# One chunk's square blocks over the two halves of the partitions, in place of block-diagonal tiles of two chunks, in a recurrent mixer

## The chip, the cores and the metric

The kernel runs on one core of a Trainium2 chip. A core has a matmul engine (PE, whose weight loads are listed as PEld), three engines for elementwise work (DVE, ACT, POOL), a queue that issues most transfers (SP), 128 partitions of on-chip memory (SBUF) and eight banks per partition for matmul results (PSUM). Each engine runs its own queue in order and waits on semaphores of the others. The metric is device microseconds (us) of one execution, the median of several runs.

## The reference, cut to what matters

A decoder block on 1024 tokens of 1024 columns in fp32: a recurrent mixer (RWKV-7, 8 heads of 64) and a differential attention (4 heads) side by side, merged by gates, then a feed-forward layer that picks 128 of 16384 experts per token. The change touches the recurrence alone:

```python
def step(state, inp):
    r_t, w_t, k_t, v_t, kk_t, a_t = inp
    sa = jnp.einsum('bhvk,bhk->bhv', state, -kk_t)
    state = (state * w_t[:, :, None, :]
             + sa[..., None] * (kk_t * a_t)[:, :, None, :]
             + v_t[..., None] * k_t[:, :, None, :])
    return state, jnp.einsum('bhvk,bhk->bhv', state, r_t)
```

The kernel computes it in chunks of 64 tokens. Within a chunk the recurrence is a unit triangular system with a 64x64 matrix A of decayed products of keys; (1 + A)^-1 turns it into matrix products, and only a 64x64 state passes from chunk to chunk.

## The kernel before, in words

**Stages.** `mix(0)` handles tokens 0 to 511, then `pick(0)` chooses their experts; `mix(1)` and `pick(1)` do the same for tokens 512 to 1023. After that `gates` and `ahead` prepare, and `dense` runs the last 512 tokens through all experts as matrix products. The first 512 tokens go through `peer`: 1024 gathers of 128 expert rows (512 KB each), issued on POOL (L795), each consumed by one DVE instruction (L817 for rows of u, L824 for rows of v). They start during `mix(1)` and go on beside `dense` to the end.

**Inside a mix.** Four calls of `rwkv(h)`, each for two heads: head 0 of the pair has its 64 features on partitions 0 to 63, head 1 on 64 to 127. Beside each call stand the input projections of the next call (matmuls `z`, L162 to L166; their weights are split in two parts by ACT, L147, and DVE, L148), one attention head and four gate columns. The order of each engine's queue is fixed when the program is built: the builder's scheduler lets projections and attention stand between the steps of the recurrence.

**One call of `rwkv`** works on W = 512 tokens: TT = 4 tiles of 128 tokens, NC = 8 chunks of 64. Elementwise products with decays give kt, rr, bT and kT. Then, for each head `hh`:
- `am` (L334, L336): A and its relatives, per 128 tokens a 128x128 product in which only the two diagonal 64x64 blocks are wanted; DVE multiplies with a mask that zeroes the rest (L338), into the tiles mb and mk.
- Diagonal 16x16 blocks of A go out to memory (`m_s`) and back with a block to a partition, DVE inverts them by 30 small steps (L379, L381), the result goes out (`z_s`) and back as the block-diagonal XT (L387). PE transposes it (`xtr`, L390) to X.
- Two doubling levels: DVE masks A (M, L357), PE makes Y (L401), ACT copies it (L403), PE makes Xn and XTn (L409, L414), DVE subtracts them (L410, L415). The two heads alternate, each with a PSUM bank and tiles of its own.
- `akv`, W, U0 (L420, L430), copied by ACT. Then per chunk parity `Pp` and `Qp` (L451 to L457); DVE writes the heads' diagonal blocks (L443) and POOL zeroes the other blocks (L442), so that Pd and Qm are again block diagonal. `rh` and `y` (L462 to L473).
- The state passes through 8 chunks: PE `y` and `sn` (L480, L489), DVE `st` (L490).

Work tiles come from a ring of NR = 22 tiles of 128x512 (`rt`), PSUM results of the mixer from three banks (`rbank`). An instruction that writes a ring tile waits until the last reader of its old contents is done.

In words of size: every fp32 product here appears in the trace as two weight loads and two matmuls; a transpose as one of each.

Of the kernel before, what the change touches and what calls it, by code (L numbers as in the profile page):

```python
# [25 lines left out]
NR = 22  # L26
# [12 lines left out]
PADB = 8 * (16 * P + 16)  # L39
# [6 lines left out]
def body(ctx: ExitStack, tc: tile.TileContext, ins, out, dbg=None):  # L46
# [24 lines left out]

    def at(name, dt=F32):
        return hp.tile([P, 512], dt, name=name, tag="at", bufs=NA)
# [10 lines left out]
    def v4(ap):  # L84
        return ap.rearrange("p (a s) -> p a s", s=P)
# [18 lines left out]
    mask2 = const("mask2", [P, 256])  # L104
    lvl = const("lvl", [P, 2, P])
# [33 lines left out]
    for i in range(4):  # L139
        nc.sync.dma_start(ins["z_s"][i // 2, i % 2].rearrange("(p s) -> p s", p=P), zero[:, 0:4 * PADB // P])  # L140

# [35 lines left out]
    def invroot(ssq, n, scale, eps, op1=OP.add, pool=None):  # L177
        """(ssq * scale + eps) ** -0.5 for [128, n] (op1 max: the larger of the two)."""
# [4 lines left out]
        # a first guess from the exponent, then Newton's steps  # L183
# [16 lines left out]
    def normed(src, w):  # L200
        """RMSNorm of rows of src, w over all partitions (two halves [128, 512] each)."""
# [10 lines left out]
    def to_cols(xn, a, hi, lo):  # L212
        """Rows of 128 tokens (two halves) to the transposed hi, lo [128, column / 128, token]."""
# [9 lines left out]
    def head_stats(sq, W, scale, eps, op1):  # L223
        """Per token and half of the partitions: (sum(sq) * scale, eps) ** -0.5, spread back over them."""
# [13 lines left out]
    def mix(gi, t0, W):  # L238
# [35 lines left out]
        def rwkv(h, kz, rz, vz):  # L274
# [38 lines left out]

            def totok(name, f):
                b = rbank("tt")[:, :W]
                for a in range(TT):
                    nc.tensor.transpose(b[:, a * P:(a + 1) * P], f[:, a * P:(a + 1) * P], ident)
# [4 lines left out]
            # A matrices, all transposed ([s, t]) and block diagonal over the chunks  # L322
            MB = [[None] * TT, [None] * TT]
            MK = [[None] * TT, [None] * TT]
            ATs = [[], []]
            for hh in range(2):
                rs = slice(64 * hh, 64 * hh + 64)
# [703 lines left out]
```

## Time and profile before

| | |
|---|---|
| median of 3 runs | 3668.87 us (3668.75 to 3677.71) |
| profiled execution, first to last instruction | 3659.9 us |
| difference of the fastest run to that span | 8.9 us |
| matmuls on PE, and weight loads | 15166 each |
| busy: PE, DVE, ACT, POOL | 3224.0, 2995.0, 1344.7, 1350.5 us |
| `rwkv` calls of mix(0): decay scan (L290) starts | 89.4, 203.6, 327.2, 452.1 us |
| `rwkv` calls of mix(1) | 835.0, 1010.2, 1188.0, 1362.8 us |
| first gated expert weights of `dense` (L887) | 2175.2 us |

A profile comes from one execution. The page of a profile lists busy time per engine, the span in 40 slices, the chain that ended last and the costliest groups of instructions. Other views list groups by line with the mean time of one, stretches of time with each engine's busy time, or single instructions in order of time. A matmul's listed length includes its way through the array, so neighbours overlap; the distance from start to start is what one costs in a row of many.

### The profile page before, as it was taken

The numbers are of one execution on the slowest core, as the hardware profiler recorded it, in microseconds if no ns is written. First come the engines' busy times: TensorE is split into PE (matmuls) and PEld (weight loads), VectorE is DVE, ScalarE is ACT, GpSimd is POOL, SyncE is SP. The second block draws the span as 40 slices with busy tenths as digits, with TensorE's granted clock in tenths as the row PEclk, the third lists the DMA queues.
The fourth block names the chain that finished last, engine by engine and source line by source line (L and its number), as shares of the span: only waits on it lengthen the run. The fifth ranks groups of instructions, "written<-read, shape, count | busy, mean of one in ns | idle before, by whom it ended". The sixth has DMA issues, their size and how long they took to land. (4 is left out here: it accounts for less than half of the span.)

```text
span 3659.9 us, 46805 instructions
## 1 busy us (share of the span) xinstructions
PE 3224.0 (88%) x15166; PEld 2571.2 (70%) x15166; DVE 2995.0 (82%) x6666; ACT 1344.7 (37%) x2497; POOL 1350.5 (37%) x1100
## 2 busy tenths in 40 slices
PE   6999989998979796678888868999999999999997
PEld 5878867776857675556665656777777777777775
DVE  4655555978889888899988758998999999999997
ACT  3333433343323342122498863322222332222332
POOL 0000000004454445552012223656566665565652
PEclk9988989997979897788989879999999999999998
DMA  4222234426676667886467888999999999999995
GB/s 138 62 72 76 73 109 152 135 79 221 226 239 231 229 235 271 314 319 207 125 207 225 263 282 316 348 340 351 349 356 351 350 351 345 347 340 352 348 351 184
DMA packets 407110, 903.24 MB, mean 247 GB/s; under 512 B 52240, under 2 KB 139088, under 8 KB 402768
## 3 DMA queue, kind: packets, MB, share of 16 engines
q0 software_dynamic: 147456, 536.94, 41.6%
q1 hardware_dynamic: 259408, 363.31, 29.3%
q8 instruction: 119, 1.95, 0.2%
q14 instruction: 127, 1.04, 0.1%
HBM read 831.41 MB, written 68.69 MB: 246 GB/s over the span
## 5 line engine op out<-in xcount | busy, mean ns | idle before, releaser
L795 POOL DMA_INDIRECT uv<-u,ids x512 | 656.7, 1283 | 1140.4 <-DVE uv L817 538.3
L795 POOL DMA_INDIRECT uv<-v,ids x512 | 673.0, 1315 | 582.4 <-DVE acc L824 416.0
L824 DVE SCALAR_TENSOR_TENSOR acc<-uv,act,acc 128x1024 f32<-128x1024 f32 x512 | 655.9, 1281 | 52.4 <-DMA uv<-v,ids 46.0
L817 DVE SCALAR_TENSOR_TENSOR uv<-uv,hb 128x1024 f32<-128x1024 f32 x512 | 617.3, 1219 | 78.2 <-DMA uv<-u,ids 77.2
L147 ACT ACTIVATE whi<-wraw 128x512 fp32r<-128x512 f32 x552 | 344.7, 630 | 741.8 <-PE z L163 252.7
L162 PE MATMUL ua<-fh,whi 128*128 128x512 f32 x1024 | 428.7, 419 | 83.4 <-DVE accd L907 68.2
L148 DVE TENSOR_TENSOR wlo<-wraw,whi 128x512 fp32r<-128x512 f32 x552 | 373.7, 686 | 155.0 <-ACT whi L147 151.3
L163 PE MATMUL ua<-fl,whi 128*128 128x512 f32 x1024 | 422.6, 413 | 0.0
L173 PE MATMUL yk<-vh,ah 128*128 128x512 f32 x768 | 304.3, 396 | 21.7 <-ACT ah L169 20.8
L174 PE MATMUL yk<-vl,ah 128*128 128x512 f32 x768 | 304.3, 396 | 10.8 <-DVE vl L170 10.8
L162 PEld LDWEIGHTS ua<-fh,whi 128*128 128x128 f32 x1024 | 204.5, 200 | 147.5 <-DVE accd L907 85.9
L169 ACT ACTIVATE ah<-gw 128x512 fp32r<-128x512 f32 x128 | 80.8, 631 | 614.0 <-DVE gw L887 614.0
L175 PE MATMUL yk<-vh,al 128*128 128x512 f32 x768 | 304.0, 396 | 0.0
L162 PE MATMUL z<-hh,whi 128*128 128x512 f32 x672 | 273.8, 408 | 1.5 <-ACT whi L147 0.9
L166 PE MATMUL ua<-fh,wlo 128*128 128x512 f32 x1024 | 266.6, 400 | 5.3 <-DVE wlo L148 5.3
L166 PE MATMUL z<-hh,wlo 128*128 128x512 f32 x672 | 270.7, 403 | 0.0
L163 PE MATMUL z<-hl,whi 128*128 128x512 f32 x672 | 270.0, 402 | 0.0
L846 PE MATMUL gb<-oh,ohg 128*128 128x128 f32 x1024 | 226.4, 342 | 40.5 <-ACT ohg L845 39.1
L846 PEld LDWEIGHTS gb<-oh,ohg 128*128 128x128 f32 x1024 | 166.1, 209 | 103.8 <-ACT ohg L845 66.5
L163 PEld LDWEIGHTS ua<-fl,whi 128*128 128x128 f32 x1024 | 204.4, 200 | 44.6
L166 PEld LDWEIGHTS ua<-fh,wlo 128*128 128x128 f32 x1024 | 195.0, 191 | 48.5 <-DVE wlo L148 5.8
L845 ACT ACTIVATE ohg<-ohb,sl 128x128 f32<-128x128 bf16 x512 | 228.1, 537 | 2.5 <-DVE ohb L840 2.4
(325 smaller groups left out, 6199.0 us busy)
## 6 DMA issues: line engine op xcount, KB each, us to landing
wraw<-ut SPq DMA_DIRECT2D x256, 256.0 KB, 6.4
vraw<-v SPq DMA_DIRECT2D x256, 256.0 KB, 6.5
wraw<-w_in SPq DMA_DIRECT2D x168, 256.0 KB, 2.7
gd_s<-st SPq DMA_DIRECT2D x16, 2048.0 KB, 11.2
gt<-gd_s SPq DMA_DIRECT2D x32, 1024.0 KB, 8.9
wraw<-wq SPq DMA_DIRECT2D x64, 256.0 KB, 2.9
g_s<-sgo SPq DMA_DIRECT2D x32, 256.0 KB, 3.1
wraw<-proj SPq DMA_DIRECT2D x32, 256.0 KB, 3.6
```

What stands on the lines that cost most here:

```text
L147: nc.scalar.activation(hi, raw, AF.Copy)
L148: nc.vector.tensor_tensor(lo, raw, hi.bitcast(F32), op=OP.subtract)
L162: nc.tensor.matmul(o, hi, xh(k), start=(k == 0), stop=False)
L163: nc.tensor.matmul(o, hi, xl(k), start=False, stop=False)
L166: nc.tensor.matmul(o, lo, xh(k), start=False, stop=(k == n - 1))
L173: nc.tensor.matmul(o, ah, bh, start=first, stop=False)
L174: nc.tensor.matmul(o, ah, bl, start=False, stop=False)
L175: nc.tensor.matmul(o, al, bh, start=False, stop=last)
L795: nc.gpsimd.indirect_dma_start(out=t, out_offset=None, in_=ins[src], in_offset=bass.IndirectOffsetOnAxis(ap=ids[:, j:j + 1], axis=0))
L817: nc.vector.scalar_tensor_tensor(u, u, 1.0, hb, op0=OP.mult, op1=OP.mult, accum_out=act[:, j:j + 1])
L824: nc.vector.scalar_tensor_tensor(acc, v, act[:, j:j + 1], acc, op0=OP.mult, op1=OP.add)
L846: nc.tensor.matmul(b[:, k * P:(k + 1) * P], o3[:, k], o1[:, k], start=True, stop=True)
```

## The change

The two heads of a call now share every tile. A square block of one chunk and one head takes 64 partitions: chunks of even number on partitions 0 to 63, odd ones on 64 to 127, and the columns hold 64 per pair of chunks and head (q = head x 4 + pair). The zero blocks are no longer stored or multiplied.

- Every 128x128x128 product of the recurrence becomes two products of 64x64x64, one in the upper half of the rows and columns of the array and one in the lower, written in turns (`rs in HC`). `am` has the same number of products, each with 64 weight columns in place of 128. `xtr` is now a product with an identity instead of a transpose.
- In `am` and `byfeat` (Pp, Qp, rh, y) the halves of the rows write to two different PSUM banks; in `each` (xtr, Y, Xn, XTn), `bytok` (akv, W, U0) and the state they write to the two halves of the partitions of one bank.
- Both heads' masks, copies and subtractions are one instruction each. Pd and Qm hold no zero blocks, and POOL's memsets are gone. The chunks' `y` is no longer summed with the state's part in PSUM: it is copied out by ACT and added by DVE.
- The ring has 16 tiles instead of 22, and a second ring `r2` has four tiles of 128x1024 (KR, MB, MK, and the merge's products).
- The scratch `m_s` and `z_s` hold 64x64 blocks; XT comes back in four transfers instead of two.

The matmul, mask and copy shapes shrink as the code below shows; comments taken out elsewhere change nothing.

```diff
-NR = 22
+NR = 16
+NR2 = 4
...
+    def r2(name):
+        return gp.tile([P, D], F32, name=name, tag="r2", bufs=NR2)
...
-            kt, rr = rt_("kt"), rt_("rr")
-            nc.vector.tensor_tensor(c3(kt), c3(kk), Ep[:, :, 0:CH], op=OP.mult)
-            nc.vector.tensor_tensor(c3(rr), c3(rz), Ep[:, :, 1:], op=OP.mult)
+            KR = r2("KR").rearrange("p (k c s) -> p k c s", k=2, s=CH)[:, :, :NC, :]
+            kt, rr = KR[:, 0], KR[:, 1]
+            nc.vector.tensor_tensor(kt, c3(kk), Ep[:, :, 0:CH], op=OP.mult)
+            nc.vector.tensor_tensor(rr, c3(rz), Ep[:, :, 1:], op=OP.mult)
...
+            HC = (slice(0, 64), slice(64, P))
+            QN = 2 * TT
+
+
+            MBK = []
+            for name, src in (("MB", bT), ("MK", kT)):
+                m = r2(name).rearrange("p (q s) -> p q s", s=P)
+                bs = [rbank("am") for _ in HC]
+                for c in range(NC):
+                    for hh, rs in enumerate(HC):
+                        nc.tensor.matmul(bs[hh][HC[c % 2], (c // 2) * P:(c // 2 + 1) * P],
+                                         src[rs, c * CH:(c + 1) * CH], KR[rs, :, c, :], start=True, stop=True)
+                for hh in range(2):
+                    nc.vector.tensor_tensor(m[:, hh * TT:(hh + 1) * TT, :], v4(bs[hh][:, :W]),
+                                            mask2[:, None, :].to_broadcast([P, TT, P]), op=OP.mult)
+                MBK.append(m)
+            MB, MK = MBK
...
-            # A matrices, all transposed ([s, t]) and block diagonal over the chunks
-            MB = [[None] * TT, [None] * TT]
...
+            flat = lambda f: lambda a: f[:, a * P:(a + 1) * P]
+            ctok = totok("ctok", lambda a: kt[:, 2 * a:2 * a + 2, :].rearrange("p c s -> p (c s)"))
...
-            nb = 8 * TT
-            full = lambda t: bass.AP(t.tensor, t.offset, [[P, P], [PADB, TT], [1, P]])
-            diag = lambda t: bass.AP(t.tensor, t.offset, [[16 * P + 16, nb], [P, 16], [1, 16]])
+            nb = 4 * NC
+            full = lambda t, par: bass.AP(t.tensor, t.offset + par * CHB, [[CH, CH], [2 * CHB, TT], [1, CH]])
+            diag = lambda t: bass.AP(t.tensor, t.offset, [[16 * CH + 16, nb], [CH, 16], [1, 16]])
             for hh in range(2):
                 m_s = ins["m_s"][h % 2, hh]
-                for i, mb in enumerate(ATs[hh]):
-                    nc.sync.dma_start(full(m_s)[:, 2 * i:2 * i + 2, :],
-                                      mb.rearrange("p (j k s) -> p j k s", j=2, k=2)[:, :, 0, :])
+                for par, rs in enumerate(HC):
+                    nc.sync.dma_start(full(m_s, par), MB[rs, hh * TT:(hh + 1) * TT, 0:CH])
                 nc.sync.dma_start(ab[hh * nb:(hh + 1) * nb], diag(m_s))
...
-            XT, X = [None, None], [None, None]
+            qv = lambda t: t[:, :QN * CH].rearrange("p (q s) -> p q s", s=CH)
+            XT = qv(rt("XT"))
...
                 nc.sync.dma_start(diag(z_s), z[hh * nb:(hh + 1) * nb])
-                XT[hh] = rt_("XT")
-                nc.sync.dma_start(v4(XT[hh]), full(z_s))
+                for par, rs in enumerate(HC):
+                    nc.sync.dma_start(XT[rs, hh * TT:(hh + 1) * TT, :], full(z_s, par))
+
+            def each(name, l, r):
+
+                b = qv(rbank(name))
+                for q in range(QN):
+                    for rs in HC:
+                        nc.tensor.matmul(b[rs, q, :], l[rs, q, :], r(rs, q), start=True, stop=True)
+                return b
+
+            at_q = lambda t: lambda rs, q: t[rs, q, :]
+            X = qv(rt("X"))
+            nc.scalar.activation(X, each("xtr", XT, lambda rs, q: eyec[rs, :]), AF.Copy)
+            for l in range(2):
+                M = qv(rt("M"))
+                nc.vector.tensor_tensor(M, MB[:, :, 0:CH], lvl[:, l:l + 1, :].to_broadcast([P, QN, CH]), op=OP.mult)
+                Y = qv(rt("Y"))
+                nc.scalar.activation(Y, each("Y", M, at_q(X)), AF.Copy)
+                if l < 1:
+                    nc.vector.tensor_tensor(X, X, each("Xn", XT, at_q(Y)), op=OP.subtract)
+                nc.vector.tensor_tensor(XT, XT, each("XTn", Y, at_q(XT)), op=OP.subtract)
+
+            def bytok(name, l, src, scale):
+                b = rbank(name)[:, :W]
                 for a in range(TT):
+                    for hh in range(2):
+                        for rs in HC:
+                            nc.tensor.matmul(v4(b)[rs, a, HC[hh]], l[rs, hh * TT + a, 0:CH], src[rs, a, HC[hh]],
+                                             start=True, stop=True)
+                t = rt_(name)
+                nc.scalar.activation(t, b, AF.Copy, scale=scale)
+                return v4(t)
+
+            AkV = bytok("akv", MK, vtok, 1.0)
+            Wt = bytok("W", XT, ctok, -1.0)
+            U0 = bytok("U0", XT, AkV, -1.0)
+
+            def byfeat(names, *terms):
+
+                bs = [rbank(names) for _ in HC]
+                o = [b[:, 0:TT * CH].rearrange("p (a s) -> p a s", s=CH) for b in bs]
                 for a in range(TT):
+                    for i, (l, r) in enumerate(terms):
+                        for hh in range(2):
+                            for par, rs in enumerate(HC):
+                                nc.tensor.matmul(o[par][HC[hh], a, :], l[rs, a, HC[hh]], r(rs, a, hh),
+                                                 start=(i == 0), stop=(i == len(terms) - 1))
+                return o
+
...
-                    nc.gpsimd.memset(v4(t)[hc, :, 64 - 64 * hh:128 - 64 * hh], 0.0)
-                    nc.vector.tensor_tensor(v4(t)[hc, :, hc], v4(b)[hc, :, hc], x(hc), op=op)
...
+            halves = lambda t: [t[:, i * TT * CH:(i + 1) * TT * CH].rearrange("p (a s) -> p a s", s=CH)
+                                for i in range(2)]
+            tok = lambda t: lambda rs, a, hh: t[rs, a, HC[hh]]
+            Pd, Qm = halves(rt("Pd")), halves(rt("Qm"))
+            for par, b in enumerate(byfeat("Pp", (Wt, tok(btok)))):
+                nc.vector.tensor_tensor(Pd[par], b, eyec[:, None, :].to_broadcast([P, TT, CH]), op=OP.add)
+            Gp = G.rearrange("p (a c) -> p a c", c=2)
+            for par, b in enumerate(byfeat("Qp", (btok, tok(U0)), (ktok, tok(vtok)))):
+                nc.vector.tensor_tensor(Qm[par], b, Gp[:, :, par:par + 1].to_broadcast([P, TT, CH]), op=OP.mult)
+            by_rr = lambda m: lambda rs, a, hh: m[rs, hh * TT + a, CH:P]
+            for par, b in enumerate(byfeat("rh", (Wt, by_rr(MB)))):
+                nc.vector.tensor_tensor(c4(rh)[:, :, par, :], rr.rearrange("p (a c) s -> p a c s", c=2)[:, :, par, :],
+                                        b, op=OP.add)
...
+            y = rt_("ysb")
+            for par, b in enumerate(byfeat("y", (U0, by_rr(MB)), (vtok, by_rr(MK)))):
+                nc.scalar.activation(c4(y)[:, :, par, :], b, AF.Copy)
+            by = rbank("ys")
...
+                    for rs in HC:
+                        nc.tensor.matmul(by[rs, c * CH:(c + 1) * CH], S[rs, :], rh[rs, c * CH:(c + 1) * CH],
+                                         start=True, stop=True)
...
+                    for rs in HC:
+                        nc.tensor.matmul(b[rs, 0:CH], Pd[c % 2][rs, c // 2, :], S[rs, :], start=True, stop=True)
+                    nc.vector.scalar_tensor_tensor(Sn, b[:, 0:CH], G[:, c:c + 1], Qm[c % 2][:, c // 2, :],
                                                    op0=OP.mult, op1=OP.add)
...
+            o = CH if gi == 0 else 0
+            nc.vector.tensor_tensor(y[:, o:], y[:, o:], by[:, o:W], op=OP.add)
...
+        mg = [r2("mg") for _ in range(4)]
...
-                t = rt_("mg") if i == 0 else sgm
+                t = mg[d // 2][:, d % 2 * 512:d % 2 * 512 + W] if i == 0 else sgm
```

How this moves the queues is seen at two places. The first is PE's queue in the second call of mix(0), from the first doubling level to U0. Rows read: line, operation, result <- operands, shape of the result, and how many in a row; `z` rows are input projections, `pT` attention. Before:

```order
L401 MATMUL Y<-X,M 128x128 x4
L409 MATMUL Xn<-Y,XT 128x128 x4
L414 MATMUL XTn<-XT,Y 128x128 x4
L409 MATMUL Xn<-Y,XT 128x128 x4
L414 MATMUL XTn<-XT,Y 128x128 x4
L401 MATMUL Y<-X,M 128x128 x4
L583 MATMUL pT<-ident,sc 128x128 x4
L401 MATMUL Y<-X,M 128x128 x4
L414 MATMUL XTn<-XT,Y 128x128 x8
L420 MATMUL akv<-vtok,mk 128x64 x8
L430 MATMUL W<-ctok,XT 128x64 x8
L430 MATMUL U_1948<-AkV,XT 128x64 x8
```

The same place of the change, from Y of the first level to U0:

```order
L390 MATMUL Y<-X,M 64x64 x16
L168 MATMUL z<-hl,whi 128x512
L171 MATMUL z<-hh,wlo 128x512
L390 MATMUL Xn<-Y,XT 64x64 x16
L390 MATMUL XTn<-XT,Y 64x64 x16
L390 MATMUL Y<-X,M 64x64 x16
L560 MATMUL pT<-ident,sc 128x128 x4
L390 MATMUL XTn<-XT,Y 64x64 x16
L410 MATMUL akv<-vtok,MK 64x64 x16
L410 MATMUL W<-ctok,XT 64x64 x16
L410 MATMUL U_2066<-akv,XT 64x64 x16
```

Each step has 16 small products for both heads where 4 larger ones for one head stood; the turns between heads (XTn of one beside Xn of the other) are gone, so that each step now stands directly behind the one whose result it needs, with two `z` matmuls or four transposes of the attention between.

The second place is POOL's queue during mix(1), where its gathers (`uv`) stand among its memsets. Before:

```order
L795 DMA uv<-u,ids 128x1024 x2
L292 MEMSET Ep 128x8
L795 DMA uv<-u,ids 128x1024 x33
L442 MEMSET Pd 64x4x64 x2
L442 MEMSET Qm 64x4x64 x2
L442 MEMSET Pd 64x4x64 x2
L442 MEMSET Qm 64x4x64 x2
L795 DMA uv<-u,ids 128x1024 x29
```

The same stretch of the change:

```order
L297 MEMSET Ep 128x8 x5
L773 DMA uv<-u,ids 128x1024 x2
L297 MEMSET Ep 128x8
L773 DMA uv<-u,ids 128x1024 x63
L297 MEMSET Ep 128x8
L773 DMA uv<-u,ids 128x1024 x62
L297 MEMSET Ep 128x8
L773 DMA uv<-u,ids 128x1024
```

The memsets of Pd and Qm, which stood between the gathers, are gone; those of Ep stay. In both orders DVE has consumed 395 of the 1024 gathers when the first gated weights of `dense` stand in its queue.

More of the change, by code (lines that the diff above doesn't have):

```diff
@@ L103, in body @@
     lora = const("lora", [P, 2, 512])
-    mask2 = const("mask2", [P, 256])
-    lvl = const("lvl", [P, 2, P])
+    mask2 = const("mask2", [P, P])
+    lvl = const("lvl", [P, 2, CH])
+    eyec = const("eyec", [P, CH])
     eye16 = const("eye16", [64, 16, 16])
@@ L139, in body @@
     for i in range(4):
-        nc.sync.dma_start(ins["z_s"][i // 2, i % 2].rearrange("(p s) -> p s", p=P), zero[:, 0:4 * PADB // P])
+        nc.sync.dma_start(ins["z_s"][i // 2, i % 2].rearrange("(p s) -> p s", p=P), zero[:, 0:8 * CHB // P])
     def wsplit(src):
@@ L316, in totok @@
                 for a in range(TT):
-                    nc.tensor.transpose(b[:, a * P:(a + 1) * P], f[:, a * P:(a + 1) * P], ident)
+                    nc.tensor.transpose(b[:, a * P:(a + 1) * P], f(a), ident)
                 t = rt_(name)
@@ L416, in rwkv @@
-            b = rbank("akv")[:, :W]
-            for hh in range(2):
-                for a in range(TT):
-                    o = slice(a * P + hh * 64, a * P + hh * 64 + 64)
-                    nc.tensor.matmul(b[:, o], MK[hh][a][:, 0:P], vtok[:, a, hh * 64:hh * 64 + 64],
-                                     start=True, stop=True)
-            AkV = rt_("AkV")
-            nc.scalar.activation(AkV, b, AF.Copy)
-            WU = []
-            for name, src in (("W", ctok), ("U0", v4(AkV))):
-                b = rbank(name)[:, :W]
-                for hh in range(2):
-                    for a in range(TT):
-                        o = slice(a * P + hh * 64, a * P + hh * 64 + 64)
-                        nc.tensor.matmul(b[:, o], XT[hh][:, a * P:(a + 1) * P], src[:, a, hh * 64:hh * 64 + 64],
-                                         start=True, stop=True)
-                t = rt_(name)
-                nc.scalar.activation(t, b, AF.Copy, scale=-1.0)
-                WU.append(v4(t))
@@ L985, in prepare @@
     a["ident"] = np.eye(P, dtype=f)
-    s = np.arange(P)[:, None]
-    t = np.arange(P)[None, :]
-    same = (s // CH) == (t // CH)
-    strict = (same & (t > s)).astype(f)
-    incl = (same & (t >= s)).astype(f)
-    a["mask2"] = c(np.concatenate([strict, incl], axis=1))
+    s = np.arange(P)[:, None] % CH
+    t = np.arange(CH)[None, :]
+    a["mask2"] = c(np.concatenate([t > s, t >= s], axis=1).astype(f))
     lv = []
@@ L995, in prepare @@
     a["lvl"] = c(np.stack(lv, axis=1).astype(f))
+    a["eyec"] = (s == t).astype(f)
+    p = np.arange(P)
+    same = (p[:, None] // CH) == (p[None, :] // CH)
     a["eye16"] = c(np.tile(np.eye(16, dtype=f)[None], (64, 1, 1)))
@@ L1011 @@
            "gd_s": (P // CE, P, 512, CE), "a_s": (NE, P, 512),
-           "m_s": (2, 2, 4 * PADB), "z_s": (2, 2, 4 * PADB)}
+           "m_s": (2, 2, 8 * CHB), "z_s": (2, 2, 8 * CHB)}
 def kernel(**inputs):
```

110 lines of the change are left out of this document (7 added, 103 removed).

## Prediction

> **What bounds the kernel now.** The page first, since it shows the stages: its head and, of its 40 slices of 91.5 us, the busy tenths and the granted clock.
>
> ```profile
> span 3659.9 us, 46805 instructions
> PE 3224.0 (88%) x15166; PEld 2571.2 (70%) x15166; DVE 2995.0 (82%) x6666; ACT 1344.7 (37%) x2497; POOL 1350.5 (37%) x1100
> PE   6999989998979796678888868999999999999997
> DVE  4655555978889888899988758998999999999997
> POOL 0000000004454445552012223656566665565652
> PEclk9988989997979897788989879999999999999998
> ```
>
> PE alone is full in the first six slices (the first mix); from the tenth on DVE is as full, because POOL's gathers need it. The mean over the span hides this, so I cut the span at the starts of the `rwkv` calls (the view of stretches: PE, PEld, DVE, ACT, POOL busy, clock, DMA share, GB/s): four calls of mix(0), two of mix(1), and the dense stage.
>
> ```profile
> 89.00:204.00 115.00, 113.11 (x683) 93.58 (x682) 64.36 (x193) 41.53 (x79) 2.56 (x9) 0.99 0.25 77
> 204.00:327.00 123.00, 118.90 (x673) 98.85 (x673) 63.94 (x192) 40.38 (x77) 2.57 (x9) 0.92 0.24 70
> 327.00:452.00 125.00, 121.45 (x684) 100.45 (x683) 65.60 (x202) 45.92 (x87) 2.57 (x9) 0.92 0.22 68
> 452.00:551.00 99.00, 84.18 (x513) 69.00 (x512) 55.82 (x159) 35.88 (x62) 2.57 (x9) 0.88 0.35 110
> 1010.00:1188.00 178.00, 148.43 (x818) 120.99 (x818) 155.47 (x428) 54.97 (x94) 87.39 (x72) 0.86 0.71 234
> 1363.00:1543.00 180.00, 122.46 (x664) 96.00 (x664) 150.48 (x247) 43.48 (x75) 95.86 (x84) 0.77 0.83 288
> 2200.00:3600.00 1400.00, 1318.70 (x5526) 1052.13 (x5525) 1300.94 (x1729) 410.36 (x709) 820.17 (x619) 0.98 0.95 345
> ```
>
> The first three calls of mix(0) are bound by PE (97 to 98% busy, DVE half idle): what PE sheds there is time won. The fourth has no projections left to fill gaps, 15 of its 99 us are idle on PE. In mix(1) DVE leads (155 of 178 us) and PE follows (148), so DVE's saving counts, at most in full. The dense stage has PE, DVE and the transfers at 93 to 95%; the change does not touch it, and since 395 gathers are consumed ahead of it in both orders, it is not handed more work: what the mixes win arrives at the end.
>
> **The change on PE.** How long a product takes in a row of many is the distance of starts in the view of single instructions:
>
> ```profile
> 136.69 1.06 PE L414 MATMUL XTn<-XT,Y 128*128 128x128 f32 x8
> 137.58 1.06 PE L409 MATMUL Xn<-Y,XT 128*128 128x128 f32 x8
> ...
> 155.71 0.44 PE L471 MATMUL y<-mb,U 128*64 128x128 f32 x4
> 155.93 0.44 PE L473 MATMUL y<-mk,vtok 128*64 128x128 f32 x4
> ...
> L414 PE MATMUL XTn<-XT,Y 128*128 128x128 f32 x256 | 33.4, 278 | 0.0
> ```
>
> Eight instructions with 128 weight columns take 0.89 us, 0.112 each; four with 64 columns 0.22, 0.055 each. The group row is L414 over all calls: 256 = 8 calls x 16 products x 2, so each fp32 product counts twice. Per call, before: am 64, xtr 8, inversion 80, akv/W/U0 48, Pp/Qp 48, together 248 x 0.112 = 27.8 us; rh and y 48 x 0.055 = 2.6; sum 30.4. After: am 64, xtr 32, inversion 160, and three times 96: 544 of 64 columns each. One behind another at 0.055 that is 29.9, no gain. But neighbours now use opposite halves of the rows, and two such streams meet once in the trace, at the end of `am`:
>
> ```profile
> 102.72 0.27 PE L334 MATMUL am<-kt,kT 64*128 64x128 f32 x1
> 102.73 0.37 PE L334 MATMUL am<-kt,bT 64*128 64x128 f32 x1
> ...
> 103.06 0.27 PE L336 MATMUL am<-rr,bT 64*128 64x128 f32 x1
> 103.06 0.27 PE L336 MATMUL am<-rr,kT 64*128 64x128 f32 x1
> 103.17 0.27 PE L336 MATMUL am<-rr,bT 64*128 64x128 f32 x1
> 103.28 0.38 PE L334 MATMUL am<-kt,bT 64*128 64x128 f32 x2
> ```
>
> Products of the two heads start within 0.01 us of each other, and eight matmuls take 0.56 us where a single stream needs 0.90: a factor of 0.62. A 64x64x64 product is not in the trace; its bounds are 0.055 (no overlap) and 0.028 (two full streams). I take 0.055 x 0.62 = 0.034, nearest to that row: 544 x 0.034 = 18.5 us, **11.9 less** per call (0.5 to 15.2). Here the trace shows overlap with two PSUM banks only.
>
> The Trainium skill speaks against part of it: TensorEngine Tiling (Array Packing), Restrictions and Gotchas, says that different row tiles cannot access one PSUM bank at the same time; `each` and `bytok` write both halves to one bank, and no run here shows that. By this rule the sum is that of the first rival below.
>
> The second and third call lose more today:
>
> ```profile
> 98.00:104.00 6.00, 5.53 (x45) 4.80 (x46) 5.54 (x15) 0.69 (x1) 0.00 (x0) 1.00 0.12 34
> 145.00:158.00 13.00, 13.00 (x138) 12.64 (x137) 4.29 (x10) 1.79 (x3) 0.61 (x2) 1.00 0.01 1
> 216.00:222.00 6.00, 6.00 (x29) 6.00 (x29) 2.67 (x5) 0.00 (x0) 0.00 (x0) 0.50 0.20 63
> 222.00:231.00 9.00, 9.00 (x46) 8.78 (x46) 4.50 (x12) 1.47 (x5) 0.00 (x0) 0.50 0.20 47
> ```
>
> There `am` runs at half the granted clock, 75 matmuls in 15 us, 0.2 each: 64 cost 12.8 instead of 7.2. After, at twice 0.034, they cost 4.4 instead of 2.2. So these calls gain 3.4 us more, 15.3.
>
> **What is late next.** Both heads now share each step, so the copy behind a step is no longer covered by the other head's products. Xn stands two projections (about 0.5 us) behind Y, XTn four transposes (0.45) behind the next Y, and the copy takes 0.6 (row of L403 below) plus the way; the second half of `am` waits for a mask (0.69), and Qp, rh and y each for the evacuation of a bank (0.42), as three banks serve products that take two. Six waits of about 0.5: 3 us per call, between 1 and 5. Behind each, PE's whole queue stands, projections too. The transfers around the 16x16 inversion are not in the sum: XT's takes 4.8 us to land, now in four smaller pieces, and projections stand in PE's queue ahead of it as before.
>
> mix(0): 11.9 - 3 = 8.9 for the first call, 12.3 for each of the next two, and for the fourth, where latency rules, half of 11.9: 6. Sum 39 us.
>
> **The change on DVE**, by the groups over all calls:
>
> ```profile
> L357 DVE TENSOR_TENSOR M<-mb,lvl 128x256 f32<-128x256 f32 x64 | 24.2, 421 | 9.3 <-PE Y L401 9.3
> L338 DVE TENSOR_TENSOR mk<-am,mask 128x512 f32<-128x512 f32 x32 | 22.1, 690 | 14.4 <-PE am L336 14.1
> L338 DVE TENSOR_TENSOR mb<-am,mask 128x512 f32<-128x512 f32 x32 | 22.0, 688 | 13.9 <-PE am L336 13.8
> L415 DVE TENSOR_TENSOR XT<-XT,XTn 128x512 f32<-128x512 f32 x32 | 21.8, 684 | 9.9 <-PE XTn L414 9.3
> L490 DVE SCALAR_TENSOR_TENSOR st<-sn,G,Qm 128x128 f32<-128x128 f32 x56 | 19.5, 348 | 33.5 <-PE sn L489 33.1
> L403 ACT ACTIVATE Y<-Y 128x512 f32<-128x512 f32 x32 | 19.0, 595 | 49.0 <-PE Y L401 45.1 <-DVE cand L718 3.9
> L443 DVE TENSOR_TENSOR Pd<-Pp,ident 64x256 f32<-64x256 f32 x32 | 13.5, 422 | 31.2 <-PE Pp L451 30.8
> L443 DVE TENSOR_TENSOR Qm<-Qp,G 64x256 f32<-64x256 f32 x32 | 13.5, 422 | 5.3 <-PE Qp L457 4.8
> L410 DVE TENSOR_TENSOR X<-X,Xn 128x512 f32<-128x512 f32 x16 | 11.0, 684 | 3.2 <-PE Xn L409 3.1
> L442 POOL MEMSET Pd<- 64x256 f32 x32 | 9.8, 306 | 237.1 <-PE Y L401 233.8 <-issue 1.0 <-PE XTn L414 0.7
> XT<-z_s SPq DMA_DIRECT2D x16, 256.0 KB, 4.8
> ```
>
> Per call (an eighth of each count): masks of `am` 8 to 4, 2.8 us saved; M 8 x 0.42 to 2 x 0.69, 2.0; X one and XT two fewer, 2.0; blocks 8 to 4 of 0.42, 1.7; seven `st` of half the width, by the slope between the 256 and 512 columns above 0.07 less each, 0.5. Added: y plus state 0.69, and rh in two pieces of 0.42 for one of 0.69, 0.15. Sum **8.1 us less**. In mix(1) DVE is busy 0.87 of the time, so I count 0.87 x 8.1 = 7 per call, 28 in all (bounds 0, if gathers set the pace, and 12 per call, if PE's saving comes on top). POOL loses its memsets, which held gathers up while they waited; counted in the code, the ring tiles that a call holds at once fall from about 21 to 9, so 16 suffice. Both count as nothing.
>
> **Sum:** 39 + 28 = 67 us. The profiled execution's own time is its span and about 9 us around it, which is the fastest run and, within 0.1 us, the median. 3668.9 - 67 = **3602**; by the bounds of its terms 3570 to 3635.
>
> **Rivals.**
> 1. Halves that share a bank take turns. Then only am and the 192 of Pp, Qp, rh, y overlap: 256 x 0.034 + 288 x 0.055 = 24.5, 5.9 less per call, with 2.5 us of waits: 3.4, 6.8, 6.8 and 3 in mix(0), 20; with 28 in mix(1) 3621. For it: the trace's overlap has two banks. Against it: the halves' results are on different partitions.
> 2. No overlap at all, or PE cannot take instructions faster than one pair in 0.055 us (no stretch of the trace is denser). 29.9 and 2 us of waits against 30.4: mix(0) plus or minus nothing, mix(1) 5 per call from DVE: 3649.
> 3. **Slower: the clock falls.** In rows 216 to 231 PE is listed as fully busy and still has 0.50 for 15 us, with 64-row products and transposes; with 128 rows (145 to 158) it keeps 1.00. If small products hold too little of the array at work, the 480 from xtr to y run at half clock: 480 x 0.068 = 32.6 instead of 23.2, and 3 of waits, less 5 to 8 won in `am`: 4 to 7 lost per call of mix(0), 20 in all; mix(1), with slack, even: 3689. Without overlap too, 480 x 0.11 = 53, 27 lost per call of mix(0) and 15 of mix(1): up to 3840. It decides from a little over half of that stretch at half clock (8.9 won against 16.3 for the whole of it). Against it: 64-row `am` keeps 1.00 in 98 to 104. The Trainium skill, TensorE: Matmul & The Clock Gate, Part 1, has the clock rise after about 3.4 us of sustained work; by that this rival has no room, but the rows of 216 to 231 differ.
> 4. More: full overlap, and mix(1) gains 12 per call: 39 + 13 + 48, 3569 or less.
>
> **Chances.** Forecast 0.49, rivals in order 0.17, 0.15, 0.13, 0.06. A range of 3565 to 3662 holds the first three and most of the fourth case, and leaves out the clock. This kernel's measurement tells about 0.3%, 11 us: faster 0.49 + 0.17 + 0.06 + 0.06 of rival 2 = 0.78, same 0.09, slower 0.13.
>
> **What would show it.** Right: starts of `each` products at about 0.034 us, calls of mix(0) at 105 to 113 us instead of 115 to 125, mix(1) calls at about 170, dense stage as long as before. Rival 1: `byfeat` near 0.034 but `each` at 0.055. Rival 2: all at 0.055. Rival 3: 0.50 in the clock between xtr and y. Wrong altogether: PE idle where XT or the merge's tiles are awaited.

## The result, and the profile after

The changed kernel takes **3570.09 us** (median of 4 runs, 3565.23 to 3577.26) against 3668.81 beside it (4 runs): ratio 0.9736, 95% interval 0.9716 to 0.9757, some 97 us less. Forecast were 3602 us and a range of 3565 to 3662: faster, as forecast, by half as much again as the 67 us of the sum. Two slow executions in the experiments below, 9840 us of `before_turns` and 7760 us of the kernel before, are left out of the ratios.

The head of the page after, with the rows of the 40 slices shown of before:

```profile
span 3564.5 us, 50945 instructions
PE 3102.8 (87%) x17382; PEld 2427.3 (68%) x17382; DVE 2929.3 (82%) x6546; ACT 1335.0 (37%) x2483; POOL 1318.3 (37%) x1036
PE   6999988998888874969888879999989999999997
DVE  4555556977989897899888678999989998999997
PEclk9999988998989886979889989999999999999999
```

PE has 2216 matmuls more and is busy 121 us less; DVE is busy 66 us less, 8.2 per call (forecast 8.1). Cut at the starts of the calls, as before (four calls of mix(0), four of mix(1), `dense`):

```profile
91.30:193.10 101.80, 99.07 (x956) 75.04 (x955) 56.16 (x178) 39.66 (x77) 0.11 (x1) 1.00 0.28 82
193.10:297.70 104.60, 100.26 (x951) 76.90 (x950) 56.51 (x177) 39.52 (x76) 0.11 (x1) 0.95 0.27 78
297.70:402.20 104.50, 99.98 (x959) 76.20 (x958) 57.92 (x187) 43.77 (x84) 0.11 (x1) 0.98 0.26 76
402.20:492.20 90.00, 71.36 (x791) 55.34 (x790) 47.84 (x145) 34.93 (x60) 0.11 (x1) 0.83 0.37 118
774.30:945.90 171.60, 141.67 (x1106) 106.51 (x1105) 143.97 (x416) 54.63 (x94) 78.50 (x62) 0.86 0.71 236
945.90:1110.20 164.30, 134.36 (x1096) 104.06 (x1096) 143.97 (x408) 54.08 (x91) 85.27 (x63) 0.85 0.75 248
1110.20:1269.90 159.70, 133.61 (x1108) 104.20 (x1109) 141.40 (x352) 60.42 (x102) 78.79 (x60) 0.88 0.75 246
1269.90:1440.90 171.00, 100.51 (x904) 75.23 (x903) 134.66 (x221) 40.15 (x71) 92.74 (x75) 0.70 0.84 288
2079.80:3530.30 1450.50, 1363.16 (x5704) 1084.80 (x5705) 1339.32 (x1785) 426.80 (x739) 818.99 (x625) 0.98 0.94 342
```

PE still fills the first three calls, and the second and third now keep 0.95 and 0.98 of the clock instead of 0.92. `dense` is as long as before: 1450.5 us in the last row, against 1449.7 between the same two instructions of the kernel before. Between the profiled executions the spans differ by 95.4 us: mix(0)'s calls give 61.0, mix(1)'s 30.5, all the rest 3.9. A call is counted up to the next call's scan, the fourth up to the merge's first sum.

| call | length before, after | changed products on PE before, after |
|---|---|---|
| mix(0), 1st | 114.2, 101.8 (-12.4) | 30.8, 18.1 (-12.7) |
| 2nd | 123.6, 104.6 (-19.0) | 37.0, 17.7 (-19.3) |
| 3rd | 124.9, 104.5 (-20.4) | 37.0, 17.1 (-19.9) |
| 4th | 99.2, 90.0 (-9.2) | 33.3, 22.4 (-10.9) |
| mix(1), four | 697.1, 666.6 (-30.5) | 144.0, 91.3 (-52.7) |

The last column sums, over am, xtr to U0, Pp, Qp, rh and y, the distances from one matmul's start to the next. In mix(0) each call is shorter by what its products lost on PE, within 1.7 us; in mix(1) little more than half of it arrives. The pace, from the view of single instructions of the first call (start, length, instruction; `each` and `bytok`, whose halves share a bank):

```profile
138.65 1.10 PE L390 MATMUL XTn<-XT,Y 64*64 64x64 f32 x32
139.67 1.15 PE L390 MATMUL Y<-X,M 64*64 64x64 f32 x32
140.75 1.05 PE L573 MATMUL hs<-ones,sq 128*128 128x2 f32 x8
...
144.47 1.15 PE L410 MATMUL W<-ctok,XT 64*64 64x64 f32 x32
145.46 1.04 PE L410 MATMUL U<-akv,XT 64*64 64x64 f32 x30
```

W's 32 instructions take 0.99 us from start to start, **0.031 each**, XTn's 1.02: the overlap that the forecast put at 0.034, and in one bank.

The forecast's bound of 0.028 does not hold where all four quarters of the array take turns, as in `byfeat`. Half of y's instructions in the second call (the other half stand among them), from the views by tile of the changed kernel, of `noturns` (for y: columns in turn, same rows) and of `notile` (one quarter); both are described below:

```profile
L428 PE MATMUL y<-MK,vtok x32: 218/218/265, 250.7 to 251.7; 64*64 64x64 f32 x32
```

```profile
L428 PE MATMUL y<-MK,vtok x32: 218/218/218, 260.3 to 261.8; 64*64 64x64 f32 x32
```

```profile
L428 PE MATMUL y<-MK,vtok x32: 218/218/218, 265.3 to 268.3; 64*64 64x64 f32 x32
```

The 64 instructions of y take 0.99, 1.64 and 3.02 us from start to start: 0.016, 0.026 and 0.047 each. Am, whose products are 128 wide, takes 0.048 each in the first call. On DVE, the groups that answer to those of before:

```profile
L403 DVE TENSOR_TENSOR XT<-XT,XTn 128x512 f32<-128x512 f32 x16 | 11.0, 686 | 13.3 <-PE XTn L390 13.3
L398 DVE TENSOR_TENSOR M<-MB,lvl 128x512 f32<-128x512 f32 x16 | 10.7, 681 | 0.0
L333 DVE TENSOR_TENSOR MB<-am,mask 128x512 f32<-128x512 f32 x16 | 10.2, 681 | 1.5 <-PE am L330 1.5
L438 DVE TENSOR_TENSOR Pd<-Pp,eyec 128x256 f32<-128x256 f32 x16 | 6.0, 418 | 10.7 <-PE Pp L428 10.7
L467 DVE SCALAR_TENSOR_TENSOR st<-sn,G,Qm 128x64 f32<-128x64 f32 x56 | 15.8, 281 | 34.9 <-PE sn L466 34.8
```

XT, MB and Pd have half the instructions at the same length each: one mask takes 0.68 for both heads. M has a quarter, each of twice the width, and st as many, each shorter.

### The profile page after: what moved, and what is told of

Its sections match the earlier page's. It is cut to its first block, busy times and chain, and to the rows that moved or that the text cites. A ratio compares the mean times of both kernels' runs of the same rounds, so it can differ in the third digit from the quotient of the medians.

```text
span 3564.5 us, 50945 instructions
## 1 busy us (share of the span) xinstructions
PE 3102.8 (87%) x17382; PEld 2427.3 (68%) x17382; DVE 2929.3 (82%) x6546; ACT 1335.0 (37%) x2483; POOL 1318.3 (37%) x1036
## 3 DMA queue, kind: packets, MB, share of 16 engines
q14 instruction: 125, 1.02, 0.1%
## 5 line engine op out<-in xcount | busy, mean ns | idle before, releaser
L773 POOL DMA_INDIRECT uv<-u,ids x512 | 644.7, 1259 | 1210.1 <-DVE uv L795 535.9
## 6 DMA issues: line engine op xcount, KB each, us to landing
gd_s<-st SPq DMA_DIRECT2D x16, 2048.0 KB, 11.9
```

The lines of the kernel that those rows point to most:

```text
L773: nc.gpsimd.indirect_dma_start(out=t, out_offset=None, in_=ins[src], in_offset=bass.IndirectOffsetOnAxis(ap=ids[:, j:j + 1], axis=0))
```

## The experiments

Below, "+x us" is the difference of two ratios to the kernel before, times 3669; intervals are 95%, and the changed kernel's own reaches 8 us to each side. Since the builder's scheduler orders the queues anew for each kernel, an edit also moves rows elsewhere: of some 10000 rows of PE in the trace (runs of equal instructions), about 90 differ from the changed kernel's in `memsets`, 600 in `noturns_bank`, 700 to 2500 in the others made from it. Differences of a few us outside the edited place prove nothing.

**Turns of the halves: all, am alone, one bank alone.** Each loop first runs over one half of the rows, then over the other, as in `each`; `noturns` has it everywhere, `noturns_am` in am alone, `noturns_bank` in each and bytok.

```diff
-                for q in range(QN):
-                    for rs in HC:
+                for rs in HC:
+                    for q in range(QN):
```

> The changed kernel with every product loop (am, each, bytok, byfeat) first over all of one half of the rows, then over all of the other; same instructions, same tiles, same work on the other engines. My theory (overlap of the two halves is what PE gains, in mix(0) above all): products go at 0.055 us each instead of 0.03, some 11 to 14 us more of PE per call, the second and third call get their half-clock stretch of about 20 us back; the four calls of mix(0) grow by 10 to 18 us each, mix(1) by 0 to 10 each: 3615 to 3650 us, 45 to 80 over the changed kernel, with PE of a call back near 30 us. Rival A (the gain comes from less work on DVE and POOL): within 10 us of the changed kernel, 3560 to 3580. Rival B (fewer waits, by fewer and larger copies): the same, 3560 to 3585.

> The changed kernel with only am's loop without turns. My theory of the clock (two halves of 64 rows at once are enough for the full clock, one is not): am goes at 0.055 us at full clock in the first call and at about 0.11 us in the second and third, where the half-clock stretch is again near 20 us long instead of 7 or less; these two calls grow by 6 to 12 us each, the first and fourth by 2 to 4: 3585 to 3600 us. Rival (the half-clock stretch went because the work ahead of am moved, not because of am's turns): the half clock stays at 7 us or less, every call of mix(0) grows by 2 to 4 us: 3578 to 3586.

> The changed kernel with only each and bytok (the products whose halves share one bank: xtr, Y, Xn, XTn, akv, W, U0, 288 of 544 instructions per call) without turns; am and byfeat keep theirs. My theory (halves overlap in one bank as they do in two): 288 x (0.055 - 0.03) = 7 us more of PE per call, 15 to 28 us in mix(0), 0 to 15 in mix(1): 3590 to 3610. Rival (in one bank the halves take turns, and the turns win nothing there): no difference, 3563 to 3578.

Measured: `noturns` 3653.62 us, ratio 0.997 (0.9948 to 0.9992), **+86**, a little over the 45 to 80 expected; `noturns_am` 3575.72, 0.9768 (0.9751 to 0.9786), +12, intervals that touch; `noturns_bank` 3655.81, 0.9993 (0.9974 to 1.0013), **+94**, more than twice what was expected. Without the turns of the 288 instructions that share a bank nearly the whole gain is gone, so the rival in which they win nothing is false. So are the rivals of `noturns`, which have the gain from DVE, POOL or fewer waits. Why so much more than pace? Here are `noturns_bank`'s single instructions where W and then U begin, in the second call and in the first:

```profile
269.80 0.27 PE L410 MATMUL W<-ctok,XT 64*64 64x64 f32 x1
271.30 0.27 PE L410 MATMUL U<-akv,XT 64*64 64x64 f32 x1
...
152.67 0.36 PE L410 MATMUL W<-ctok,XT 64*64 64x64 f32 x1
155.35 0.36 PE L410 MATMUL U<-akv,XT 64*64 64x64 f32 x1
```

Without turns W takes 1.50 us, 0.047 each, in the second call, and 2.68 in the first. The stretches of the same run with their clock (third number from the right); its profiled execution is one of its slower ones, 19 us over its median:

```profile
136.00:164.00 28.00, 28.00 (x360) 27.17 (x361) 3.92 (x8) 5.74 (x10) 0.00 (x0) 0.50 0.03 11
252.00:276.00 24.00, 23.35 (x423) 20.28 (x421) 7.92 (x19) 6.11 (x12) 0.00 (x0) 1.00 0.10 27
```

Pace alone lengthens the second and third call by 6.8 and 8.4 us; where the clock falls in the inversion it stays at 0.50 through the chain with PE full, and the first and fourth call lose 21.3 and 15.0. From Y's first start to Qp's last, this run needs 17.8 to 18.4 us in the three calls that keep the clock and 27.7 to 31.8 in the other five, there all but 2 us of it at half clock; the changed kernel needs 11.7 to 17.2, of which at most 8.5 are at half clock, and the kernel before 20.1 to 23.6, all but 2 us of it in one call at full. Three calls of mix(1) are so longer by 17 to 24 us. That is rival 3 of the prediction, which the turns keep away.

`noturns_am` missed from the other side: am lost nothing (2.9 us for 64 in the first call, 3.1 in the changed kernel). The chunks in turn still alternate the halves of the *columns*. That gave the next cut.

**One quarter of the array.** am and byfeat ordered so that neighbours share rows and columns (byfeat likewise by par, then hh):

```diff
-                for c in range(NC):
-                    for hh, rs in enumerate(HC):
+                for hh, rs in enumerate(HC):
+                    for c in [*range(0, NC, 2), *range(1, NC, 2)]:
```

> The changed kernel with am and byfeat (256 of 544 instructions per call) ordered so that neighbours use one quarter of the array, the same rows and the same columns, as each and bytok did in noturns_bank; in noturns, am and byfeat still had neighbours on the other half of the columns and kept their pace. Theory (it is the change of the array's quarter that lets neighbours overlap, by rows or by columns alike): am 64 x (0.10 - 0.045) = 3.5 us more per call, byfeat 192 x (0.048 - 0.026) = 4 us, and the clock falls in some calls: 3600 to 3645. Rival (am and byfeat are not bound by the pace of their products but by banks and copies): 3565 to 3585.

Measured 3608.94 us, 0.9855 (0.9819 to 0.989), **+44**: the theory. Am of the first call, in `noturns_am` (columns in turn) and in `notile`:

```profile
101.20 1.26 PE L330 MATMUL am<-KR,bT 64*64 64x128 f32 x26
...
104.11 0.44 PE L341 MATMUL tt<-ident,KR 128*128 128x128 f32 x2
```

```profile
102.56 2.24 PE L330 MATMUL am<-KR,bT 64*64 64x128 f32 x29
...
107.03 0.44 PE L341 MATMUL tt<-ident,KR 128*128 128x128 f32 x2
```

64 instructions take 2.91 us with columns in turn and 4.47 in one quarter; y takes 3.0 instead of 1.0 to 1.4. In the second call am, and the transposes behind it, stay at half clock for the whole of a stretch of `notile`, 8.3 us for am alone:

```profile
210.30:224.00 13.70, 13.70 (x85) 12.21 (x84) 5.66 (x15) 3.39 (x9) 0.00 (x0) 0.50 0.18 43
```

**The kernel before, with turns.** Am, Pp and Qp write in turns over the row halves, into two banks; 128 weight columns as before. Am's core:

```diff
-                        b = rbank("am")
+                    bs = [rbank("am") for _ in range(2)]
...
+                        for i, x in enumerate((kt, rr)):
+                            for hh in range(2):
+                                rs = slice(64 * hh, 64 * hh + 64)
+                                nc.tensor.matmul(bs[hh][:, 256 * j + 128 * i:256 * j + 128 * i + 128], src[rs, cs],
+                                                 x[rs, cs], start=True, stop=True)
```

> The kernel before, with only am, Pp and Qp in turns over the two halves of the rows (both halves' banks open at once); tiles, masks, inversion and everything else as before. Theory (a turn over tiles of the array that share neither rows nor bank wins the same with 128 columns): am 64 x (0.112 - 0.06) = 3.3 us per call, Pp and Qp 48 x 0.05 = 2.4 us, and the second and third call of mix(0) lose most of the 20.5 us at half clock, 7 us each: mix(0) 35 us shorter, mix(1) 0 to 15: 3610 to 3640. Rival (the overlap needs both halves of the columns as well, products of 128 columns fill them and win nothing): within 8 us of the kernel before, half clock in calls 2 and 3 as before.

Measured 3640.66 us, 0.9903 (0.9866 to 0.994): by the ratio 36 us less than before (22 to 49), at the edge of what was expected. The medians differ by 24 and the profiled spans by 21, so it is a quarter to a third of the change's gain, with none of its tiles. The pace is not where it comes from: only Pp reaches the 0.06 us that was expected (0.062 each), while Qp stays at 0.098, and am hardly shrinks in the first call (6.3 instead of 7.0 us). That call is 3.2 us shorter, the second and third 8.3 and 9.9. In the second the clock is back 4.4 us after am's start at 213.4:

```profile
211.00:217.80 6.80, 6.38 (x35) 4.91 (x36) 4.82 (x14) 1.57 (x5) 0.00 (x0) 0.50 0.23 62
217.80:224.00 6.20, 5.54 (x53) 4.91 (x51) 4.16 (x10) 1.56 (x3) 0.00 (x0) 1.00 0.28 68
```

The stretches at half clock around am of the second and third call, with am's own time:

| kernel | neighbours in am | half clock, us | am, us |
|---|---|---|---|
| before | same rows, all columns | 20.5, 20.5 | 13.3, 13.3 |
| notile | same quarter | 13.7, 13.7 | 8.3, 8.3 |
| before_turns | rows in turn, all columns | 6.8, 3.4 | 8.2, 7.7 |
| noturns_am | columns in turn | 6.8, 6.8 | 4.4, 4.3 |
| changed | rows and columns in turn | 6.8, 3.4 | 4.1, 3.5 |
| memsets (below; PE's loops as changed) | rows and columns in turn | 0, 3.4 | 3.1, 3.6 |

With turns the clock returns while am runs; without, only behind am and tt, though PE is listed as full (the rows above, and 216 to 231 in the prediction).

**What the clock follows.** All lengths in the third column are whole multiples of 3.41 us, and so is each of the 1676 stretches at one clock inside the 14 profiles: the clock changes only on a grid of 3.41 us, which lies differently in each run. What the clock of a window goes with can be read from the window ahead of it. Count each matmul there at 0.112 us per 128 columns of width (0.23 for a projection), times the share of the array's rows and columns that it uses; call the sum array time. Take all windows at half clock in which PE is listed as over 99% busy. With less than 1.0 us of array time, 139 of 161 were followed by half clock again; with 1.4 us or more, 515 of 517 by full clock; between these, 72 of 141. By the same count (an estimate from the rows above) am of the kernel before does 1.7 us in a window at full clock and 0.9 at half, so that once slow it stays slow; `notile`'s does 0.7 at half, `noturns_am`'s 1.4. W does 1.5 us at full clock with turns, 1.0 without, and 0.6 without turns at half clock. So turns win twice, by pace and by the clock that the pace keeps. The counts are an agreement over windows; no run sets where the work lies on the grid.

**Work that holds the clock.** `noturns_bank`, in mix(1) alone with products of 128x128x512 ahead of the steps of the inversion (five before xtr, one before each other), into the bank that the step then overwrites; their results are not used.

```diff
+                for _ in range(0 if gi == 0 else 5 if name == "xtr" else 1):
+                    nc.tensor.matmul(b, blk, lora[:, 0, :], start=True, stop=True)
```

> The kernel of noturns_bank, with additional products of 128 rows, 128 columns and 512 wide, into the bank that the step overwrites after, in mix(1) alone: five ahead of xtr, while XT's transfer is awaited, and one ahead of each later step of the inversion. mix(0) is left as in noturns_bank. Theory (noturns_bank lost half by pace and half by the clock, which single small products do not bring back): the stretches of 40 us and more at half clock go from mix(1)'s inversions, xtr to rh takes 25 us instead of 38 in PE time, and mix(1) is shorter by 15 to 40 us in spite of some 9 us of additional products per call: 3615 to 3640. Rival (the clock only shows the waiting, and the pace is all): the half clock stays or mix(1) is longer by the additional products, 3655 to 3690.

Measured 3657.99 us, 0.9987 (0.9957 to 1.0017; 10 runs from 3631.73 to 3683.05): no difference that can be told. In the profiled execution one of mix(1)'s chains instead of three ran at half clock, which fits the theory; but that execution is the fastest of the ten, 26 us under their median, so whether the extra work costs what the clock wins stays open. This run shows something else, though: PE and DVE run the same instructions in the same order as in `noturns_bank` until mix(1), and yet the first call took 106.0 us against 123.1. The stretch of `noturns_warm`:

```profile
136.00:159.00 23.00, 22.52 (x490) 20.45 (x487) 5.66 (x14) 6.43 (x12) 0.00 (x0) 1.00 0.07 25
```

In `noturns_bank` a window of the grid ends at 136.1, where the half clock begins: it holds xtr's last products, a wait of 0.7 us, Y and the first of pT, 0.8 us of array time. In `noturns_warm` the grid cuts the same instructions elsewhere, and the two windows over them hold 1.4 (projections still among it) and 0.9. That may be the whole difference; it is not shown.

**DVE's saving undone.** Operations that write the same result again, some 8.5 us per call: in `dve_double` where the kernel before had its additional ones (Pd and Qm twice too), in `dve_one` all at the first M (13 times).

```diff
-                for hh in range(2):
+                for hh in (0, 0, 1, 1):
...
-                nc.vector.tensor_tensor(M, MB[:, :, 0:CH], lvl[:, l:l + 1, :].to_broadcast([P, QN, CH]), op=OP.mult)
+                for _ in range(4):
+                    nc.vector.tensor_tensor(M, MB[:, :, 0:CH], lvl[:, l:l + 1, :].to_broadcast([P, QN, CH]), op=OP.mult)
```

> The changed kernel with DVE's saving undone by repeats of operations that write the same result again: per call 4 masks of am (128x512), 6 M (128x512) and 4 blocks of Pd and Qm (128x256), some 8.6 us of DVE, in the places where the kernel before had its additional ones; PE's products unchanged. My theory (mix(1) gains by DVE, mix(0) by PE): mix(1) grows by about 0.87 x 8.6 = 7.5 us per call, 30 in all; in mix(0), where DVE is half idle, the repeats only lengthen the chain behind each step, 0 to 5 us per call: 3595 to 3625, most of it in mix(1). Rival A (DVE is not what bounds mix(1); PE's saving won there): mix(1) grows by less than 8 us in all. Rival B (DVE's saving won in mix(0) too): mix(0) grows by 25 us or more.

> The changed kernel with the same additional work for DVE as in dve_double (12 operations of 128x512, some 8.3 us per call), all in one place: the first level's mask M, written 13 times while XT's transfer is awaited, instead of behind each step of the chain. Theory (DVE's saving counted in mix(0) because it shortens the chain of steps on which PE waits, and in mix(1) because DVE is busy there): mix(0) grows by 0 to 2 us per call instead of the 5.4 of dve_double, mix(1) by 4 to 7 per call: 3585 to 3605. Rival (busy time of DVE is what counts everywhere): as dve_double, 3595 to 3610, of which 20 us in mix(0). Rival (latency alone counts): 3568 to 3580.

Measured: `dve_double` 3601.63 us, 0.9824 (0.9797 to 0.9851), **+32**, within the range, but in the wrong place: by the profile mix(0)'s calls grow by 21.7 us and mix(1)'s by 20.0. Its first calls of mix(0) and of mix(1):

```profile
90.50:198.20 107.70, 104.39 (x956) 78.97 (x955) 63.47 (x191) 39.23 (x76) 0.11 (x1) 0.95 0.26 78
793.90:969.20 175.30, 143.58 (x1107) 108.11 (x1105) 149.67 (x426) 55.05 (x94) 78.15 (x61) 0.83 0.69 228
```

In the first call PE has the same 956 products, is busy 5.3 us longer, and the clock has gone from 1.00 to 0.95: it falls behind a window in which PE waits 1.7 of 3.41 us, against 0.9 us in the changed kernel. `dve_one` missed: 3628.71 us, 0.9886 (0.9866 to 0.9906), +55, with 24 us in mix(0). There Y of the first call starts at 147.5 us instead of 135.5, since M is ready so late, and the order built for it puts projections ahead of Y (DVE's rows, then PE's):

```profile
134.20 7.95 DVE L399 TENSOR_TENSOR M<-MB,lvl 128x512 f32<-128x512 f32 x11
...
145.71 1.41 DVE L399 TENSOR_TENSOR M<-MB,lvl 128x512 f32<-128x512 f32 x2
...
147.21 0.40 PE L167 MATMUL z<-hh,whi 128*128 128x512 f32 x1
147.54 1.15 PE L390 MATMUL Y<-X,M 64*64 64x64 f32 x32
```

So DVE being half idle in mix(0) did not make its work there free: a step that PE's chain waits for counts, wherever it stands. How much of the 55 is the new order and how much the wait stays open.

**POOL's memsets put back**, on ring tiles that nothing reads:

```diff
+            for name in ("Pd", "Qm", "Pd", "Qm"):
+                t = rt_(name + "z")
+                for hh in range(2):
+                    nc.gpsimd.memset(v4(t)[HC[hh], :, HC[1 - hh]], 0.0)
```

> The changed kernel with POOL's memsets of before put back (8 of 64x256 per call on ring tiles that nothing reads, about 2.5 us of POOL per call, and each waits for its ring tile). My theory (they count as nothing): 3563 to 3578, mix(1) within 4 us. Rival (gathers stood behind the waiting memsets on POOL, and their removal won part of mix(1)): mix(1) and what follows 8 us longer or more, 3580 or over.

Measured 3572.49 us, 0.975 (0.972 to 0.9781): no cost that can be told, as counted.

**Faster than both.** `bonus_later` moves the bonus product and bv behind am (five lines, unchanged); `warm` puts four products of 128x128x512 ahead of xtr in the last call of mix(0) and in mix(1), results unused; `bonus_warm` does both.

```diff
-            nc.tensor.matmul(bb, blk, av, start=True, stop=True)
...
             MB, MK = MBK
+            nc.tensor.matmul(bb, blk, av, start=True, stop=True)
```

> The changed kernel with the bonus product (bb, which waits for DVE's av, and ahead of which PE waits about 4 us in the second and third call) and its multiplication bv moved behind am. A try for a faster kernel: am can start without that wait, 0 to 4 us per call of mix(0), and the clock is not halved ahead of am: 3555 to 3572. Rival: DVE's masks come later by the same wait, or am waits for kT as long as bb did for av: 3565 to 3580, no difference.

> The changed kernel with four additional products of 128x128x512 ahead of xtr, while XT's transfer is awaited, in the last call of mix(0) and in mix(1), where the steps Y, Xn and XTn behind that wait run at half clock (Y 4.5 us instead of 2.2). Theory (work ahead of the chain holds the clock): the half clock goes from these steps, 2 to 4 us per call in five calls, of which DVE lets through half: 3555 to 3570. Rival (the additional products stand in the way when XT has landed): 3570 to 3590.

> The changes of bonus_later and warm together: the sum of both, 3545 to 3570 if both win, else 3565 to 3585.

Measured: `bonus_later` **3551.52** us, 0.968 (0.966 to 0.9699), 21 less; `warm` 3583.4, 0.9764 (0.9745 to 0.9782), no gain; `bonus_warm` **3540.02**, 0.9658 (0.9641 to 0.9676), 29 less than the changed kernel and 125 less than before. The waits of PE in the second call (line, what it waited for, us in total, times, longest), of the changed kernel and of `bonus_later`:

```profile
PE bb L316 <- DVE kz L268: 3.4, 1, 3.4
```

```profile
PE am L325 <- DVE bT L309: 1.2, 1, 1.2
PE ys L456 <- DVE st L467: 0.8, 2, 0.4
PE am L325 <- DVE kT L313: 0.6, 1, 0.6
PE bb L334 <- DVE av L332: 0.3, 1, 0.3
```

Three waits of 2.1 us together stand for one of 3.4, and that call keeps the full clock (100.6 us instead of 104.6). But `memsets`, with the bonus product where it was, keeps it too:

```profile
193.20:293.90 100.70, 97.00 (x952) 74.58 (x951) 56.42 (x178) 39.73 (x76) 2.57 (x9) 1.00 0.27 81
```

The wait for the bonus product (2.8 us there) lies across two windows of the grid in both. In `memsets` these hold over 1.5 us of array time each, in the changed kernel 0.9. So the full clock of this call is not shown to come from the move. In the profiled executions the four calls of mix(0) give 7.4 us (8.0 in `memsets`) and those of mix(1) 20.5, while 16 are lost again behind them: that the kernel is faster is measured, why is open. Why `warm` costs alone and seems to win beside the other move is open: both reorder a sixth or more of PE's rows.

## Why the prediction was right, and where it was off

**Right: the sign, the mechanism, the bounds.** The gain rests on the overlap of neighbours: without the turns of the halves (`noturns`) 86 of 97 us are gone. That PE's share in the first call comes out so near (12.7 less, forecast 11.9) is partly luck. One pace of 0.034 stood for all products; the products of `each` and `bytok` go at 0.031, but am takes 3.1 us instead of 2.2, and Qp and y 1.2 and 1.4 instead of 2.2 each, with all four quarters in turn. `dense` is as long as before, the memsets count as nothing, DVE's saving is 8.2 us per call.

**Mis-sized: mix(0), 39 forecast, 61 measured.** Three terms. "Six waits of about 0.5: 3 us per call" did not arrive: the first call is shorter by 12.4 where its products lost 12.7, and PE's time idle in it went from 1.9 to 2.7 us only. That DVE's halved steps paid for the waits is likely, since undoing them costs this call 5.9 us (`dve_double`), but it is not shown apart. "So these calls gain 3.4 us more": they gained 6.6 and 7.2 more, since the clock returns during am instead of behind tt (am 4.1 and 3.5 instead of the 4.4 forecast, from 13.3 by starts instead of 12.8; with the grid's place, am of the second call takes 3.1 in `memsets`), besides 1.7 in tt, which the sum left out. The fourth call gained 9.2, not 6.

**Right sum, wrong reason: DVE.** "In mix(1) DVE is busy 0.87 of the time, so I count 0.87 x 8.1 = 7 per call, 28 in all", and none in mix(0). The calls of mix(1) gave 30.5; but `dve_double` puts the worth of DVE's saving at 20 there and 22 in mix(0). The step that failed is that an engine half idle gives nothing away: its operations stand in the chain on which PE waits. And mix(1) is no stage of DVE alone: `noturns_bank`, with DVE's work unchanged, loses 62 us in it by its profile.

**The rivals.** 1 (halves that share a bank take turns) is false by the rows of W and XTn: 0.031 us where one quarter alone needs 0.047 (`noturns`). The Trainium skill, TensorEngine Tiling (Array Packing), Restrictions and Gotchas, says that different row tiles cannot access one PSUM bank at the same time; taken as rival 1 takes it, that gives 3621, and the trace does not agree (two diagonal quarters, writing different partitions of one bank, at 0.031). Whether the shared bank costs a part is untested, since no run has this pair in two banks. 2 (no overlap) is false too; one quarter alone needs 0.047, less than the bound of 0.055. 3 (the clock) has a real mechanism with the wrong condition. The products fall to half clock and mostly stay there when neighbours share a quarter, 3656 us in `noturns_bank`; with turns the changed kernel falls too, but for at most 8.5 us of a chain. The Trainium skill, TensorE: Matmul & The Clock Gate, Part 1, has the clock rise after about 3.4 us of sustained work; am with turns agrees (3.4 us in the second call), am and tt of `notile` and of before, listed as busy for 12 and 16 us at 0.50, do not. 4 (full overlap, and 12 per call in mix(1)) gave 3569, all but the measured time, by a split that did not come: 52 us in mix(0) and 48 in mix(1), where 61 and 30.5 were measured.

## What to carry to other kernels

Where products use a half or a quarter of the array, order them so that neighbours use different rows or different columns: it is an edit of a loop, it was worth 86 us here and 21 to 36 in the kernel before, and much of it came by the clock, which a table of pace does not show. Four quarters in turn are better than two. A stage in which one engine is full is not one in which the others are free: ask of each operation whether the full engine waits for its result, not how busy its own engine is.

## What the runs showed of the hardware

- Neighbouring 64x64 products overlap when they differ in rows or in columns. Per instruction 64 wide at full clock: 0.047 us in one quarter, 0.031 in two diagonal quarters that share a bank, 0.026 in two with the same rows, 0.016 in all four (y).
- PE listed as full does not mean that the clock rises: 28 us at 0.50 in `noturns_bank`. The clock changes on a grid of 3.41 us and goes with the array time of the window before: 139 of 161 busy windows at half clock with under 1.0 us stayed at half, 515 of 517 with 1.4 us or more went to full.
- One and the same sequence of instructions ran once at half clock and once at full clock, 17 us apart in one call (`noturns_bank`, `noturns_warm`); ten runs of either kernel spread by 26 and 51 us, four of the changed kernel by 12.
